# Stick-breaking attention on one core: the mask of the diagonal tiles moves from a matmul into the scores to two elementwise products on the weights

## The chip, the cores and the metric

The kernel runs on one core of a Trainium2 chip. The engines that matter are PE (matmul), DVE (VectorE), ACT (ScalarE) and POOL (GpSimd); SP issues the DMAs. Each engine works through its own instructions in order and waits on semaphores of the others. The metric is the time of one execution in microseconds (us), the median of three runs. The profile is of one further execution, and the prediction's sum is made against that execution's own time.

## The reference, cut to what matters

A layer normalises 2048 tokens (with 16 meta tokens ahead of them), projects them to many channels, and runs three mixers side by side: a stick-breaking attention, a gated delta rule and an HGRN2. Their outputs are gated, projected and added to the input. The change touches the attention alone:

```python
z = einsum('bhqd,bhkd->bhqk', q_block, k[:q1]) * scale
mask = (s_idx < t_idx) & key_valid
log_keep = where(mask, log_sigmoid(-z), 0.0)
log_passed = cumsum(log_keep, reverse=True) - log_keep
attn = where(mask, exp(log_sigmoid(z) + log_passed), 0.0)
out = einsum('bhqk,bhkd->bhqd', attn, v)
```

Each key takes the share sigmoid(z) of what the later keys left over; what a key leaves is the remainder sigmoid(-z). A key at or after the query takes nothing (weight 0) and leaves everything (remainder 1).

## The kernel before

**Tiling.** The tokens are worked in four quarters of 512 (`j` = 0 to 3), four heads in each. Every projection is a sum of three matmuls per 128 rows (`mm3`, L175 to L178: high times high, high times low, low times high), in a 4-byte format, mostly 128x512. These projections (tiles `acc`, from `proj` and `branch`) are the bulk of PE's work and depend on little; below they are called the dense work.

**Attention.** `sb_scan` (L504) does one head of one quarter. Its inner generator `weights` makes one tile for each of the four blocks of 128 queries (`i`) against a range of keys: scores `z` into PSUM (three matmuls), two sigmoids on ACT (L525 the remainders `pc`, L526 the weights `at`), a running product from the last key to the first (L531, a scan on DVE; the next range of keys goes on from its first column, which POOL copies, L530), and the product of weights and scan (L537, on DVE for even `i`, on POOL for odd `i`). Then `values` transposes the four products on PE (L559, tile `tr`), ACT and DVE split them in high and low (L570, L127 through L571), and PE multiplies them with the values (tile `av`). At the end `put_ob` multiplies with the gate (L399) and makes the head's output `ob` (L402), which the branch product (`acc<-ob,w`) needs.

**The mask before.** Where a tile ends with the 128 keys of its own queries (`diag`, one tile per block of queries, 4 in a head, 64 in all), a fourth matmul (L522) adds -1e30 to the scores of the keys at or after the query: `ident_b` times `neg_b`, both bf16, 128x128.

**Order.** `weave` mixes an attention head (or a scan of the other mixers) with steps of dense work as the code is written out; then a scheduler that runs when the kernel is built sets the order of each engine's instructions anew, by its own estimate of how long each takes. So a change of some instructions also moves others on every engine. The buffers are fixed pools: 4 PSUM tiles for `z` and `tr` together, 21 slots "S" for the attention's tiles.

Of the kernel before, what the change touches and what calls it, by code (L numbers as in the profile page):

```python
# [7 lines left out]
F32 = mybir.dt.float32  # L8
F32R = mybir.dt.float32r
BF16 = mybir.dt.bfloat16  # L10
AF = mybir.ActivationFunctionType
ALU = mybir.AluOpType
# [3 lines left out]
P = 128  # L16
# [23 lines left out]
def kernel(  # L40
# [21 lines left out]
    nc = tc.nc  # L62

    const = ctx.enter_context(tc.tile_pool(name="const", bufs=1))
# [19 lines left out]
    def slot(tag, shape=(P, WQ), dt=F32, bufs=None):  # L84
        return pool.tile(list(shape), dt, tag=tag, name=nm(tag), bufs=bufs or BUFS[tag])
# [18 lines left out]
    def p_z():  # L104
        return ps_z.tile([P, 512], F32, tag="z", name=nm("z"))
# [7 lines left out]
    def cload(shape, src, name, dt=F32, eng=None):  # L113
        t = const.tile(list(shape), dt, name=name)
        (eng or nc.sync).dma_start(t, src)
        return t

    nw = cload([P, KC], norm_w, "nw", eng=nc.scalar)
    ident = cload([P, P], c_ident, "ident", eng=nc.scalar)
# [55 lines left out]
    def mm3(dst, lh, ll, rh, rl, first, last):  # L175
        nc.tensor.matmul(dst, lh, rh, start=first, stop=False)  # L176
        nc.tensor.matmul(dst, lh, rl, start=False, stop=False)  # L177
        nc.tensor.matmul(dst, ll, rh, start=False, stop=last)  # L178
# [325 lines left out]
    def sb_scan(j, h, st):  # L504

        qh, ql, kh, kl, vh, vl, vm0, rq, gate = st.pop(h)
# [4 lines left out]
        def weights(s, lo, hi, skh, skl, ats):  # L511
            for i in range(NT):
                e = min(hi, META + (i + 1) * P) if s == j else hi
                if e <= lo:
                    continue
                n = e - lo
                z = p_z()
                diag = s == j and e == META + (i + 1) * P
                qs = slice(META + i * P, META + (i + 1) * P)
                mm3(z[:, :n], qh[:, qs], ql[:, qs], skh[:, lo:e], skl[:, lo:e], True, not diag)  # L520
                if diag:
                    nc.tensor.matmul(z[:, n - P : n], ident_b, neg_b, start=False, stop=True)  # L522
                pc = slot("S")
                at = slot("S")
                nc.scalar.activation(pc[:, :n], z[:, :n], AF.Sigmoid, scale=rq[:, NT + i : NT + i + 1])  # L525
                nc.scalar.activation(at[:, :n], z[:, :n], AF.Sigmoid, scale=rq[:, i : i + 1])  # L526
                if carry[i] is None:
                    nc.gpsimd.memset(pc[:, n : n + 1], 1.0)
                else:
                    nc.gpsimd.tensor_copy(pc[:, n : n + 1], carry[i][:, 0:1])  # L530
                nc.vector.tensor_tensor_scan(  # L531
                    pc[:, 0:n][:, ::-1], pc[:, 0:n][:, ::-1], zero1.broadcast_to([P, n]),
                    1.0 if carry[i] is None else pc[:, n : n + 1], ALU.mult, ALU.add,
                )
                carry[i] = pc
                eng = nc.gpsimd if i % 2 else nc.vector
                eng.tensor_mul(at[:, :n], at[:, :n], pc[:, 1 : n + 1])  # L537
                ats[i] = at
                yield 0.4 + n * 0.0045
# [41 lines left out]
        for s in range(j, -1, -1):  # L581
            vm = vm0
            if s == j:
                skh, skl, svh, svl = kh, kl, vh, vl
            else:
                cs = 0 if s == 0 else META
                skh = slot("S", dt=F32R)
                skl = slot("S", dt=F32R)
# [10 lines left out]
            for lo, hi in [(META + 2 * P, WQ), (0, META + 2 * P)] if s == 0 else [(META, WQ)]:  # L599
                ats = {}  # L600
                now = weights(s, lo, hi, skh, skl, ats)
                if before is None:
                    yield from now
                else:
                    yield from alternate(now, before)
                if lo == 0:
                    work.append((lo, ats, 0, 32, None))
                for kt in range(NT):
                    if lo <= META + kt * P < hi:
                        work.append((lo, ats, META + kt * P, P, kt))  # L610
                if s == j == 0 and lo > 0:
                    continue
                if s == j:
                    work.sort(key=lambda w_: -1 if w_[4] == 0 else (0 if w_[4] is None else w_[4]))
                before = values(s, work, svh, svl, vm, lo == 0)
                work = []
# [818 lines left out]
    with tc.issue_after(marks["act"]), tc.issue_after(marks["dve"]), tc.issue_after(marks["pool"]):  # L1435
        neg32 = slot("D")
# [7 lines left out]
        lbl = cload([P, H], lb_logits, "lbl")  # L1444
        h_on = cload([P, 1], hg_on, "h_on")

        ident_b = const.tile([P, P], BF16, name="ident_b")
        nc.vector.tensor_copy(ident_b, ident)
        neg_b = const.tile([P, P], BF16, name="neg_b")
        nc.vector.tensor_copy(neg_b, neg32[:, :P])  # L1450
        ident4 = const.tile([P, NT, P], F32, name="ident4")
        for n in range(NT):
            nc.gpsimd.tensor_copy(ident4[:, n], ident)
# [153 lines left out]
```

## Time and profile before

| | |
|---|---|
| three runs | 2731.2, 2731.36, 2727.7 us; median 2731.2 us |
| the profiled execution | 2731.59 us; from its first to its last instruction 2729.8 us |
| granted TensorE clock | 0.998 of full speed |
| busy | PE 99%, DVE 52%, ACT 35%, POOL 26% |

PE counts as busy where any matmul is under way; consecutive matmuls overlap in the records, so the time that a matmul takes from PE is the distance from its start to the next start, not its duration. An idle time in brackets names what ended it.

### The profile page before, as it was taken

How to read it: one execution, taken by the hardware profiler on the slowest of the kernel's cores; microseconds unless marked ns; L12 is line 12 of the kernel's file. 1: busy time of each engine (PE TensorE's matmuls, PEld its weight loads, DVE VectorE, ACT ScalarE, POOL GpSimd, SP SyncE). 2: the span in 40 equal slices, each digit the busy share in tenths (PEclk: the TensorE clock that was granted, in tenths of full speed). 3: DMA queues.
4: the chain of work that ended last, by engine and by line, in shares of the span. 5: the costliest groups of instructions: out<-in, count | busy, mean ns of one | idle time of the engine just before them, and what ended most of it. 6: DMA issues, size and time to landing. Idle time of an engine off the chain costs nothing.

```text
span 2729.8 us, 46703 instructions
## 1 busy us (share of the span) xinstructions
PE 2693.7 (99%) x17984; PEld 2245.8 (82%) x17984; DVE 1433.1 (52%) x2878; ACT 960.2 (35%) x2207; POOL 718.8 (26%) x990
## 2 busy tenths in 40 slices
PE   7999999999999999999999999999999999999999
PEld 7998788888888888888888888888888887787887
DVE  5466647745357634443255765553325568556422
ACT  5564343343346212212144641321214456313120
POOL 4555213333133401112122332111212233302111
PEclk9999999999999999999999999999999999999999
DMA  7677756679654654557755456355764454554556
GB/s 261 221 235 251 250 184 221 231 268 319 197 180 146 206 176 130 157 160 242 230 188 171 156 171 203 107 156 155 253 217 142 163 169 142 161 161 121 162 162 212
DMA packets 201986, 521.08 MB, mean 191 GB/s; under 512 B 42976, under 2 KB 47008, under 8 KB 201764
## 3 DMA queue, kind: packets, MB, share of 16 engines
q1 hardware_dynamic: 201476, 518.03, 59.1%
q8 instruction: 142, 2.33, 0.3%
q14 instruction: 80, 0.66, 0.1%
q10 hardware_dynamic: 288, 0.07, 0.0%
HBM read 397.57 MB, written 120.44 MB: 190 GB/s over the span
## 4 chain that ended last, share of the span: by engine, by line
PE 93%; DVE 4%; DMA 1%; ACT 1%; issue 1%; POOL 0%; SPq 0%; DVEq 0%; POOLq 0%; ACTq 0%
PE acc L176 20%; PE acc L177 20%; PE acc L178 20%; PE av L176 5%; PE av L177 5%; PE av L178 5%; PE tr L559 2%; PE t L381 2%; PE z L1152 1%; PE z L176 1%; PE z L177 1%; PE z L178 1%; PE tr L381 1%; PE z L856 1%; PE tr L1237 1%
## 5 line engine op out<-in xcount | busy, mean ns | idle before, releaser
L176 PE MATMUL acc<-xh,w 128*128 128x512 f32 (+2 forms) x2096 | 796.8, 380 | 5.6 <-DVE y L1285 1.7
L177 PE MATMUL acc<-xl,w 128*128 128x512 f32 (+2 forms) x2096 | 790.7, 377 | 0.3 <-DVE xl L261 0.3
L178 PE MATMUL acc<-xh,w 128*128 128x512 f32 (+2 forms) x2096 | 787.1, 376 | 0.5 <-DVE w L127 0.5
L176 PEld LDWEIGHTS acc<-xh,w 128*128 128x128 f32 x2096 | 396.6, 189 | 75.2 <-DVE y L1285 2.1
L178 PEld LDWEIGHTS acc<-xh,w 128*128 128x128 f32 x2096 | 396.6, 189 | 66.8 <-DVE w L127 0.7
L177 PEld LDWEIGHTS acc<-xl,w 128*128 128x128 f32 x2096 | 396.4, 189 | 65.0 <-DVE xl L261 1.1
L531 DVE TENSOR_TENSOR_SCAN S<-S,zero 128x128 f32<-128x128 f32 (+4 forms) x216 | 199.1, 924 | 115.3 <-ACT S L525 105.1
L127 POOL TENSOR_TENSOR w<-wraw,w 128x512 fp32r<-128x512 f32 x106 | 147.0, 1390 | 236.2 <-ACT w L156 227.7
L537 POOL TENSOR_TENSOR S<-S,S 128x256 f32<-128x256 f32 (+2 forms) x108 | 96.5, 893 | 366.6 <-DVE S L531 196.6
L176 PE MATMUL av<-xh,w 128*128 128x512 f32 (+2 forms) x440 | 172.7, 392 | 0.0
L177 PE MATMUL av<-xl,w 128*128 128x512 f32 (+2 forms) x440 | 171.8, 390 | 0.0
L178 PE MATMUL av<-xh,w 128*128 128x512 f32 (+2 forms) x440 | 171.3, 389 | 0.0
L156 ACT CAST w<-wraw 128x512 fp32r<-128x512 f32 x182 | 112.5, 619 | 143.7 <-PE acc L178 69.9
L525 ACT ACTIVATE S<-z,rq 128x128 f32<-128x128 f32 (+4 forms) x216 | 117.1, 542 | 117.7 <-PE z L178 90.6
L737 DVE SCALAR_TENSOR_TENSOR D<-D,cw,D 128x512 f32<-128x512 f32 (+1 forms) x144 | 119.7, 838 | 21.3 <-ACT D L735 19.8
L127 DVE TENSOR_TENSOR S<-tr,S 128x512 fp32r<-128x512 f32 (+4 forms) x176 | 105.9, 606 | 42.5 <-ACT S L564 24.0
L1289 POOL TENSOR_TENSOR y<-y,g 128x512 f32<-128x512 f32 x32 | 48.2, 1506 | 288.8 <-DVE g L1287 288.8
L176 PE MATMUL acc<-ob,w 128*128 128x512 f32 x296 | 118.2, 400 | 1.4 <-ACT ob L402 1.4
L177 PE MATMUL acc<-ob,w 128*128 128x512 f32 x296 | 117.7, 398 | 0.0
L178 PE MATMUL acc<-ob,w 128*128 128x512 f32 x296 | 117.5, 397 | 0.0
L526 ACT ACTIVATE S<-z,rq 128x128 f32<-128x128 f32 (+4 forms) x216 | 116.8, 541 | 0.0
L133 POOL TENSOR_SCALAR nu<-nv 128x8 f32<-128x8 f32 (+3 forms) x39 | 14.8, 379 | 334.9 <-DVE nv L1057 194.4
(404 smaller groups left out, 4980.3 us busy)
## 6 DMA issues: line engine op xcount, KB each, us to landing
w<-wk SPq DMA_DIRECT2D x555, 512.0 KB, 3.6
wk<-w SPq DMA_DIRECT2D x184, 512.0 KB, 3.5
wraw<-in_w_in_dram SPq DMA_DIRECT2D x142, 256.0 KB, 4.0
D<-in_xq_dram SPq DMA_DIRECT2D x56, 256.0 KB, 4.4
S<-rows SPq DMA_DIRECT2D x48, 256.0 KB, 5.1
S<-dv SPq DMA_DIRECT2D x48, 256.0 KB, 4.7
out_dram<-D SPq DMA_DIRECT2D x32, 256.0 KB, 4.7
S<-dk SPq DMA_DIRECT2D x24, 264.0 KB, 3.9
```

The lines of the kernel that those rows point to most:

```text
L127: (eng or nc.gpsimd).tensor_sub(out_, a, hi.bitcast(F32))
L156: nc.scalar.copy(hi, raw)
L176: nc.tensor.matmul(dst, lh, rh, start=first, stop=False)
L177: nc.tensor.matmul(dst, lh, rl, start=False, stop=False)
L178: nc.tensor.matmul(dst, ll, rh, start=False, stop=last)
L381: nc.tensor.transpose(pt[:, n * P : (n + 1) * P], src[:, META + n * P : META + (n + 1) * P], ident)
L525: nc.scalar.activation(pc[:, :n], z[:, :n], AF.Sigmoid, scale=rq[:, NT + i : NT + i + 1])
L526: nc.scalar.activation(at[:, :n], z[:, :n], AF.Sigmoid, scale=rq[:, i : i + 1])
L531: nc.vector.tensor_tensor_scan(pc[:, 0:n][:, ::-1], pc[:, 0:n][:, ::-1], zero1.broadcast_to([P, n]), 1.0 if carry[i] is None else pc[:, n ...
L537: eng.tensor_mul(at[:, :n], at[:, :n], pc[:, 1 : n + 1])
L559: nc.tensor.transpose(tr[:kw, i * P : (i + 1) * P], ats[i][:, a - lo : a - lo + kw], ident)
L737: nc.vector.scalar_tensor_tensor(dst[:, c0:], raw[:, c0 + i : c0 + i + n], cw[:, ci, i : i + 1], dst[:, c0:], ALU.mult, ALU.add)
```

## The change

The fourth matmul is gone, and the third of the scores closes the sum. After the sigmoids, DVE takes the maximum of the last 128 columns of the remainders and a constant that is 1 at the masked keys (`later01`), and POOL multiplies the last 128 columns of the weights by its complement (`upto01`). The two constants are 4-byte tiles made once at the start, in place of the two bf16 ones.

```diff
@@ sb_scan / weights
-                mm3(z[:, :n], qh[:, qs], ql[:, qs], skh[:, lo:e], skl[:, lo:e], True, not diag)
-                if diag:
-                    nc.tensor.matmul(z[:, n - P : n], ident_b, neg_b, start=False, stop=True)
+                mm3(z[:, :n], qh[:, qs], ql[:, qs], skh[:, lo:e], skl[:, lo:e], True, True)
                 pc = slot("S")
                 at = slot("S")
                 nc.scalar.activation(pc[:, :n], z[:, :n], AF.Sigmoid, scale=rq[:, NT + i : NT + i + 1])
                 nc.scalar.activation(at[:, :n], z[:, :n], AF.Sigmoid, scale=rq[:, i : i + 1])
+                if diag:
+
+                    nc.vector.tensor_tensor(pc[:, n - P : n], pc[:, n - P : n], later01, ALU.max)
+                    nc.gpsimd.tensor_mul(at[:, n - P : n], at[:, n - P : n], upto01)
@@ constants at the start
-        ident_b = const.tile([P, P], BF16, name="ident_b")
-        nc.vector.tensor_copy(ident_b, ident)
-        neg_b = const.tile([P, P], BF16, name="neg_b")
-        nc.vector.tensor_copy(neg_b, neg32[:, :P])
+        later01 = const.tile([P, P], F32, name="later01")
+        nc.vector.tensor_scalar(later01, neg32[:, :P], -1.0, 1.0, ALU.mult, ALU.min)
+        upto01 = const.tile([P, P], F32, name="upto01")
+        nc.vector.tensor_scalar(upto01, later01, -1.0, 1.0, ALU.mult, ALU.add)
```

The lines behind the edit move by two: after the change the scan is L533, the product L539, the transposing matmul L561.

Where the instructions stand now is shown at three places. The first is DVE at the start of the second head of the second quarter (`S_1690`, `S_1699` and `S_1702` are the remainders of query blocks 0, 1 and 2, `S_1691` and `S_1703` the weights that DVE multiplies). Before:

```order
L531 SCALAR_TENSOR_TENSOR S_1690_8694<-S_1690_8694,zero1_417 128x128
L537 TENSOR_TENSOR S_1691_8695<-S_1691_8695,S_1690_8694 128x128
L531 SCALAR_TENSOR_TENSOR S_1699_8720<-S_1699_8720,zero1_417 128x256
L531 SCALAR_TENSOR_TENSOR S_1702_8738<-S_1702_8738,zero1_417 128x384
L537 TENSOR_TENSOR S_1703_8739<-S_1703_8739,S_1702_8738 128x384
```

And after, on DVE at the same place:

```order
L527 TENSOR_TENSOR S_1690_8713<-S_1690_8713,later01_408 128x128
L533 SCALAR_TENSOR_TENSOR S_1690_8713<-S_1690_8713,zero1_417 128x128
L527 TENSOR_TENSOR S_1699_8740<-S_1699_8740,later01_408 128x128
L539 TENSOR_TENSOR S_1691_8714<-S_1691_8714,S_1690_8713 128x128
L533 SCALAR_TENSOR_TENSOR S_1699_8740<-S_1699_8740,zero1_417 128x256
L527 TENSOR_TENSOR S_1702_8759<-S_1702_8759,later01_408 128x128
L533 SCALAR_TENSOR_TENSOR S_1702_8759<-S_1702_8759,zero1_417 128x384
L539 TENSOR_TENSOR S_1703_8760<-S_1703_8760,S_1702_8759 128x384
```

A maximum stands ahead of each scan, and nothing else was put between.

The second place is PE at the start of the second head of the last quarter, behind the scores of query blocks 1 to 3 (`z_4136`, `z_4139`, `z_4142`); `acc` tiles are dense work, and `tr_4152` is the first transposed tile of the head. Before:

```order
L178 MATMUL z_4142_21758<-D_4002_21211,D_3973_21095 128x512
L522 LDWEIGHTS ident_b_408
L522 MATMUL z_4142_21758<-neg_b_410,ident_b_408 128x128
L176 MATMUL acc_4293_22347<-xh_3927_20844,w2_4292_22345 128x512
L177 MATMUL acc_4293_22347<-xl_3928_20845,w2_4292_22345 128x512
L178 MATMUL acc_4293_22347<-xh_3927_20844,w2_4292_22345 128x512
L381 MATMUL t_4316_22450<-ident_83,D_4253_22197 128x128 x4
L176 MATMUL acc_4329_22486<-xh_3885_20578,w2_4327_22482 128x512
L177 MATMUL acc_4329_22486<-xl_3886_20579,w2_4327_22482 128x512
L178 MATMUL acc_4329_22486<-xh_3885_20578,w2_4327_22482 128x512
```

After, on PE (`S_4138` is the product for query block 1, made on POOL):

```order
L178 MATMUL z_4136_21781<-D_4002_21263,D_3973_21144 128x256
L176 MATMUL z_4139_21797<-D_4002_21263,D_3972_21143 128x384
L177 MATMUL z_4139_21797<-D_4003_21264,D_3972_21143 128x384
L178 MATMUL z_4139_21797<-D_4002_21263,D_3973_21144 128x384
L176 MATMUL z_4142_21813<-D_4002_21263,D_3972_21143 128x512
L177 MATMUL z_4142_21813<-D_4003_21264,D_3972_21143 128x512
L178 MATMUL z_4142_21813<-D_4002_21263,D_3973_21144 128x512
L177 MATMUL acc_4293_22404<-xl_3928_20893,w2_4292_22402 128x512
L178 MATMUL acc_4293_22404<-xh_3927_20892,w2_4292_22402 128x512
L176 MATMUL z_4149_21840<-S_4145_21832,D_3972_21143 128x512
L561 MATMUL tr_4152_21854<-ident_83,S_4129_21762 128x128
L561 MATMUL tr_4152_21854<-ident_83,S_4138_21786 128x128
```

The first two transposing matmuls now stand two dense matmuls behind the scores; before, 25 dense ones and four transposes of another tile stood there (the rows above show the first of them).

The third place is PE near the end of the last head of the last quarter, around the score tile `z_4542`, which five more follow. Before, one 128x512 matmul of a long row of dense work ahead of it, and what follows:

```order
L178 MATMUL acc_4741_24356<-xh_3927_20844,w2_4740_24354 128x512
L381 MATMUL t_4747_24403<-ident_83,D_4716_24226 128x128 x4
L176 MATMUL z_4542_23351<-S_4521_23283,D_4288_22340 128x256
L177 MATMUL z_4542_23351<-S_4522_23284,D_4288_22340 128x256
L178 MATMUL z_4542_23351<-S_4521_23283,D_4289_22341 128x256
L176 MATMUL av_4440_22947<-S_4534_23318,S_4491_23150 128x512
L177 MATMUL av_4440_22947<-S_4535_23319,S_4491_23150 128x512
L178 MATMUL av_4440_22947<-S_4534_23318,S_4492_23151 128x512
```

After, on PE at the same place:

```order
L177 MATMUL z_4526_23357<-S_4522_23348,D_4288_22397 128x256
L178 MATMUL z_4526_23357<-S_4521_23347,D_4289_22398 128x256
L177 MATMUL z_4536_23386<-S_4522_23348,D_4288_22397 128x256
L178 MATMUL z_4536_23386<-S_4521_23347,D_4289_22398 128x256
L178 MATMUL acc_4748_24476<-ob_4438_22996,w2_4736_24399 128x512
L176 MATMUL z_4542_23415<-S_4521_23347,D_4288_22397 128x256
L177 MATMUL z_4542_23415<-S_4522_23348,D_4288_22397 128x256
L178 MATMUL z_4542_23415<-S_4521_23347,D_4289_22398 128x256
L176 MATMUL av_4440_23007<-S_4534_23382,S_4491_23214 128x512
L177 MATMUL av_4440_23007<-S_4535_23383,S_4491_23214 128x512
L178 MATMUL av_4440_23007<-S_4534_23382,S_4492_23215 128x512
```

Before, 17 dense matmuls and the four transposes of `t_4747` stand between the last matmul of `z_4526` and the end of the head; after, one dense matmul does. The other 16, the four transposes and five transposes of the attention's own stand ahead of it.

## Rows read from the trace of the kernel before

**Rows 1.** The page's first part: busy time of each engine, its share of the span, instructions.

```profile
span 2729.8 us, 46703 instructions
PE 2693.7 (99%) x17984; PEld 2245.8 (82%) x17984; DVE 1433.1 (52%) x2878; ACT 960.2 (35%) x2207; POOL 718.8 (26%) x990
```

**Rows 2.** The page's fourth part: the chain of work that ended last, by engine.

```profile
PE 93%; DVE 4%; DMA 1%; ACT 1%; issue 1%; POOL 0%; SPq 0%; DVEq 0%; POOLq 0%; ACTq 0%
```

**Rows 3.** All instructions of line 522, the mask: engine, operation, count, shortest, median and longest duration in ns; below, who waited for it (us, times).

```profile
L522 PE MATMUL z<-neg_b,ident_b x64: 229/230/234, 56.5 to 2275.8; 128*128 128x128 bf16 x64
...
  ACT S L525: 22.7, 11
```

**Rows 4.** PE's instructions in order of time around two masks, in the first quarter and in the last: start in us, duration, line, tiles, shape.

```profile
58.79 0.28 PE L178 MATMUL z<-D,D 128*128 128x256 f32 x1
58.91 0.23 PE L522 MATMUL z<-neg_b,ident_b 128*128 128x128 bf16 x1
58.95 0.48 PE L176 MATMUL acc<-xh,w 128*128 128x512 f32 x1
59.27 0.39 PE L177 MATMUL acc<-xl,w 128*128 128x512 f32 x1
59.50 0.39 PE L178 MATMUL acc<-xh,w 128*128 128x512 f32 x1
...
2275.51 0.40 PE L178 MATMUL z<-D,D 128*128 128x512 f32 x1
2275.75 0.23 PE L522 MATMUL z<-neg_b,ident_b 128*128 128x128 bf16 x1
2275.79 0.48 PE L177 MATMUL acc<-xl,w 128*128 128x512 f32 x1
2276.11 0.39 PE L178 MATMUL acc<-xh,w 128*128 128x512 f32 x1
```

**Rows 5.** PE in order of time where a transposing matmul follows the mask (the last of the masks of a head of the first quarter).

```profile
88.84 0.23 PE L522 MATMUL z<-neg_b,ident_b 128*128 128x128 bf16 x1
88.91 0.27 PE L483 MATMUL t<-ident,D 128*16 128x128 f32 x1
88.94 0.48 PE L176 MATMUL acc<-xh,w 128*128 128x512 f32 x1
```

**Rows 6.** Groups of instructions by line, engine, operation and shape: busy us, mean ns of one, idle time before them and what ended it. The steps of an attention tile, and the one POOL operation that reads 128x128.

```profile
L537 DVE TENSOR_TENSOR S<-S,S 128x128 f32<-128x128 f32 x16 | 4.6, 289 | 1.7
L531 DVE TENSOR_TENSOR_SCAN S<-S,zero 128x256 f32<-128x256 f32 x64 | 47.4, 741 | 41.2 <-ACT S L525 37.8 <-ACT S L526 3.3
L525 ACT ACTIVATE S<-z,rq 128x256 f32<-128x256 f32 x64 | 30.7, 480 | 58.0 <-PE z L178 35.7 <-PE z L522 19.5 <-PE av L177 2.0
L537 POOL TENSOR_TENSOR S<-S,S 128x256 f32<-128x256 f32 x40 | 32.9, 823 | 165.5 <-DVE S L531 68.8 <-ACT S L525 54.7 <-ACT D L418 13.8
L1453 POOL COPY ident<-ident 128x128 f32<-128x128 f32 x4 | 1.4, 402 | 0.0
```

**Rows 7.** The 108 products of weights and scan on POOL, all shapes: shortest, median and longest duration in ns.

```profile
L537 POOL TENSOR_TENSOR S<-S,S x108: 632/674/1483, 60.6 to 2335.8; 128x256 f32<-128x256 f32 x40, 128x512 f32<-128x512 f32 x36, 128x272 f32<-128x272 f32 x32
```

**Rows 8.** Busy time in stretches of the span: length, then busy us (instructions) of PE, PEld, DVE, ACT, POOL, then granted clock, DMA share, GB/s. The first two rows are the last two heads of the last quarter, the third the end of the last of them, then the attention of the third, second and first quarter.

```profile
2200.00:2274.00 74.00, 72.62 (x377) 59.62 (x377) 59.95 (x93) 45.03 (x93) 25.69 (x44) 1.00 0.47 152
2274.00:2350.00 76.00, 70.02 (x363) 56.27 (x362) 58.91 (x93) 43.64 (x94) 27.36 (x42) 0.98 0.43 138
2321.87:2342.30 20.43, 17.55 (x91) 13.30 (x89) 13.09 (x23) 11.88 (x29) 3.43 (x10) 0.92 0.31 91
1355.00:1620.00 265.00, 265.00 (x1377) 220.04 (x1377) 163.13 (x266) 137.61 (x285) 71.39 (x142) 1.00 0.52 171
700.00:890.00 190.00, 190.00 (x1014) 158.91 (x1013) 116.40 (x200) 100.07 (x217) 55.96 (x109) 1.00 0.54 172
56.00:188.00 132.00, 131.94 (x944) 122.40 (x944) 71.84 (x128) 76.82 (x178) 71.15 (x96) 1.00 0.67 229
```

**Rows 9.** PE in order of time, its waits near the end of the third head of the last quarter; in brackets the idle time and what ended it.

```profile
2254.67 0.50 PE L177 MATMUL av<-S,S 128*128 128x512 f32 x1 [0.46 <-DVE S L127]
...
2256.70 0.66 PE L381 MATMUL t<-ident,D 128*128 128x128 f32 x4 [0.69 <-ACT D L759]
...
2257.90 0.50 PE L177 MATMUL av<-S,S 128*128 128x512 f32 x1 [0.23 <-DVE S L127]
```

**Rows 10.** The same for the end of the last head of the last quarter, PE and DVE, from the scan that follows `z_4526` (2321.87) on.

```profile
2321.87 0.74 DVE L531 TENSOR_TENSOR_SCAN S<-S,zero 128x256 f32<-128x256 f32 x1
...
2325.58 0.75 DVE L531 TENSOR_TENSOR_SCAN S<-S,zero 128x256 f32<-128x256 f32 x1 [0.56 <-ACT S L525]
...
2328.86 0.75 DVE L531 TENSOR_TENSOR_SCAN S<-S,zero 128x256 f32<-128x256 f32 x1 [1.40 <-ACT S L525]
...
2336.01 1.03 PE L559 MATMUL tr<-ident,S 128*32 128x128 f32 x6 [0.76 <-DVE S L537]
...
2339.04 0.67 PE L548 MATMUL av<-S,vmp 96*128 96x512 f32 x1 [2.00 <-ACT S L566]
...
2342.30 0.69 DVE L399 TENSOR_TENSOR S<-av,D 128x512 f32<-128x512 f32 x1 [2.84 <-PE av L178]
...
2343.69 0.73 PE L176 MATMUL acc<-ob,w 128*128 128x512 f32 x2 [1.43 <-ACT ob L402]
...
2349.30 0.50 PE L176 MATMUL acc<-xh,w 128*128 128x512 f32 x1 [1.71 <-DVE y L1285]
```

## The prediction

> **What bounds the kernel now.** I read the page's busy times first, then the chain of waits, then the mask's own line, then PE in order of time. PE is busy for 2693.7 of 2729.8 us, the next engine for half [rows 1], and 93% of the chain that ended last is PE [rows 2]. Through the attention of the first three quarters PE is busy in every microsecond but 0.06 (132 of 132, 190 of 190, 265 of 265 us), while DVE stays near 60% and POOL under 55% [rows 8]. There a matmul that goes is time that goes, and a delay on another engine costs nothing as long as dense work stands in front of the matmul that waits. In the last quarter this ends: in the stretch of the third head PE misses 1.4 us and in that of the fourth 6.0 us, with DVE at 60 of 74 and 59 of 76 us [rows 8]. Its waits there name DVE and ACT: three at the end of the third head [rows 9], and at the end of the fourth 0.76, 2.00, 1.43 and 1.71 us, when the dense work that needs nothing from the attention has run out [rows 10]. So the change has to be priced twice: by what PE no longer does, and by what its new order does to the last quarter.
>
> **What goes.** The 64 masks have a duration of 0.23 us each [rows 3], but matmuls overlap, so I take distances from start to start. In the first quarter the score's last matmul starts at 58.79, the mask at 58.91, the next dense matmul at 58.95 and the one behind it at 59.27 [rows 4]. From 58.79 to 59.27 are 0.48 us. Without a mask the 128x256 matmul takes 0.12 (58.79 to 58.91) and a dense one 0.23 (59.27 to 59.50), together 0.35: the mask costs 0.13 us, of which only 0.04 are its own slot and 0.09 are lost by the matmul behind it. In the last quarter 2275.51 to 2276.11 is 0.60 us against two times 0.23, 0.14 by these rounded starts [rows 4]. I take 0.13. In five of the 64 places a transposing matmul follows, and mask and transpose together take 0.10 us (88.84 to 88.94) [rows 5]; I book nothing there. 59 times 0.13 is 7.7 us. All of it stands on the chain, except where PE waits anyway, which is near none of the masks: they stand at the starts of heads, from 56.5 to 2275.7 [rows 3], and the waits at their ends. The bounds are 64 times 0.04 = 2.6 us, if the next matmul lost its 0.09 for another reason (a change of weights that comes anyway), and 64 times 0.13 = 8.3 us.
>
> The Trainium skill, page "TensorE: Matmul & The Clock Gate", section "Back-to-back issue gap", gives about 81 ns for a 128-column matmul with its weight load in a stream. By it the masks would give back 64 times 0.081 = 5.2 us; the rows show 130 ns where a 2-byte matmul stands between 4-byte ones, and I go by the rows.
>
> **What comes, and what hides it.** DVE gets 64 maxima of 128x128, both inputs in SBUF: 0.29 us each by the product of the same shape [rows 6], 18.5 us in all. POOL gets 64 products of 128x128. The trace has none of that shape: a copy of it took 0.40, a product of twice the columns 0.82 on the mean [rows 6]; nearer to both is 0.5, 32 us in all. On a path a diagonal tile gets longer by the maximum, 0.3 us, since POOL's mask runs while DVE scans for 0.74 [rows 6]; where the scan is not what POOL's product waits for, up to 0.8. ACT in turn starts earlier by the mask's 0.04 to 0.13. In the first three quarters the cover is dense work: by the new order of PE and the spacings of rows 4, at least 5 us of matmuls stand between a diagonal tile's scores and its first transpose, against a path of two sigmoids, maximum, scan and product, 0.48 + 0.29 + 0.74 + 0.82 = 2.3 us and the hops between them. I cost it at nothing; without that cover it would be 0.3 to 0.8 us per head. The two constants at the start replace two DVE instructions by two: nothing.
>
> **What moves.** In the last quarter three places count.
>
> First, the start of the second head. Behind the last score matmul of query block 1 there now stand only three of 384 columns, three of 512, two dense ones and one score matmul ahead of the two transposes: 3 times 0.17 (my estimate, three quarters of 0.23), 6 times 0.23, 1.9 us. The path to `S_4138` on POOL is the 2.3 us above plus the matmul's drain and the hops, some 2.8 us. PE waits about 0.8 us where it did not before. Bounds: 0, if the hops are short, and 2, if POOL comes late.
>
> Second, the end of the third head: its waits of 0.46, 0.69 and 0.23 us [rows 9] lie in a stretch into which the new order puts 16 dense matmuls (3.7 us). I take 1.2 us back; bounds 1.4 and minus 1 (the same waits at other instructions).
>
> Third, the end of the last head. In the new order 16 dense matmuls (3.7 us) and nine transposes (1.0 us) that stood within it stand ahead of it, so its last six tiles start 4.7 us later against the rest of the order. In return the path through them is no longer held up. From the scan at 2321.87 to the last product at 2342.30 are 20.4 us. DVE is busy for 13.1 of them [rows 8], and of its waits two at the end stay (for the last transposes, and 2.84 for the `av` matmuls). The hold-ups that can go are DVE's 1.40 before the scan of 2328.86, which waits for scores behind nine dense matmuls, 0.56 of the same kind at the scan of 2325.58, and, my estimate, about 0.5 ahead of 2321.87 [rows 10]. That is 2.5 us back for 4.7 us later: 2.2 us lost. Bounds: 0, if all of it comes back, and 4.7, if nothing does. The granted clock is 0.92 of full in this stretch against 1.00 before it [rows 8]; the waits that go before its fall are the ones that stay, so I add nothing for it.
>
> The sum: -7.7 - 1.2 + 0.8 + 2.2 = -5.9 us, on the profiled 2731.59 us, which makes 2725.7. The profiled execution lies 0.4 us above the median of 2731.2, so against the median I forecast 2725.3 us, 0.22% less. A measurement of this kernel can tell about 0.2%, 5.5 us, from no change, so the forecast lies just beyond that mark.
>
> **Rivals.** *The order takes most of it back.* The last head loses its full 4.7, the second its 2, and the third's waits come back: -7.7 + 4.7 + 2 = -1 us, 2730. For it: PE waits there already [rows 10], and the order is made by an estimate that did not foresee these waits. Against it: DVE's waits in rows 10 do show a hold-up that the move ends.
>
> *PE gains more.* The masks' full 8.3 us, the third head's 1.4, no loss at the end: -9.7 us, 2721.5. For it: in most of the span nothing else waits. Against it: 4.7 us of filler do leave a stretch that has nothing to fill it.
>
> *Slower: DVE and POOL get in each other's way.* POOL's products of one kind range from 632 to 1483 ns, at three shapes, but the median is 674 with a third of them 512 wide [rows 7], and the mean for 256 columns, 823, is above that for the median of all: POOL's time does not follow the size alone. If the new maximum and the new POOL mask, which start within a sigmoid of each other on each of the 64 tiles, each wait out the other, the path of a diagonal tile grows by 0.3 + 0.5 + 0.3 = 1.1 us. In the last quarter, where DVE is at 80%, 16 tiles would put 17 us on four heads, and the first 6 or so would vanish behind dense work: -7.7 + 11 + 2 = +5, 2736. It decides from the point at which the heads of the last quarter finish 8 us later against the dense work. Against it: the masks stand at a head's start, where the dense work is thickest. The Trainium skill speaks for this rival: "SBUF — State Buffer", section "Who interferes with whom", says that a DVE instruction with two SBUF inputs contends with a GpSimd instruction that reads SBUF, and that the later of the two waits out the other; the spread of POOL's durations agrees, though no row here shows two such instructions against each other.
>
> That the masks don't go can be left out: the new order has no L522.
>
> **How the numbers follow.** My forecast, with its own range of 2722 to 2729, gets 0.62; the order that takes it back 0.19; the greater gain 0.10; slower 0.09. Of the forecast's 0.62 two thirds lie beyond the mark of 0.2%, which with the greater gain gives 0.51 for faster. The rest of the forecast and the order that takes it back give 0.40 for no difference, and 0.09 is left for slower. The range goes from 2719, below the greater gain since the masks' cost is read from a few starts, to 2732, which takes in the order that takes it back and leaves out most of the slower rival.
>
> **What would show it.** Right: PE's busy time falls by some 8 us; behind `z`'s third matmul of a diagonal tile the next starts with no 0.09 lost; the maxima take 0.29 us; in the first three quarters PE stays busy throughout; the wait of the last head's end grows from 6 to about 8 us in all. Wrong: PE idle in the first three quarters behind transposes that wait for L539 on POOL; POOL's masks longer than 0.8 us; or the last head's end no later, or 5 us later, against the dense work.

## The result: 0.26% slower, and the profile after

The changed kernel takes 2736.1 us, the median of 11 runs, against 2729.0 for the kernel before on the same chip: a ratio of 1.0026, with a 95% interval of 1.0018 to 1.0034. That is 7.2 us more, where 5.9 less had been forecast; 2736.1 lies outside the range of 2719 to 2732.

Busy times and chain of the page after, for [rows 1] and [rows 2]:

```profile
span 2734.3 us, 46658 instructions
PE 2690.1 (98%) x17920; PEld 2242.8 (82%) x17920; DVE 1466.2 (54%) x2942; ACT 959.1 (35%) x2207; POOL 745.4 (27%) x1054
...
PE 90%; DVE 6%; DMA 1%; ACT 1%; issue 1%; POOL 1%; SPq 0%; DVEq 0%; POOLq 0%; ACTq 0%
```

PE works 3.6 us less and waits 8.1 us more (44.2 against 36.1 us idle in the span); DVE's share of the chain grew. The stretches of [rows 8] tell where:

```profile
2200.00:2274.00 74.00, 71.90 (x371) 59.12 (x370) 56.43 (x87) 41.02 (x83) 21.57 (x40) 1.00 0.45 144
2274.00:2350.00 76.00, 64.28 (x316) 50.45 (x315) 55.98 (x91) 41.95 (x87) 23.85 (x40) 0.96 0.37 116
...
1355.00:1620.00 265.00, 264.83 (x1372) 220.49 (x1372) 170.14 (x282) 136.78 (x283) 77.42 (x155) 1.00 0.52 170
...
700.00:890.00 190.00, 190.00 (x1007) 159.64 (x1006) 128.18 (x223) 100.25 (x219) 67.04 (x129) 1.00 0.53 173
...
56.00:188.00 132.00, 131.08 (x934) 121.31 (x933) 82.80 (x146) 76.58 (x175) 81.83 (x112) 1.00 0.67 229
```

In the first three quarters PE stays busy to within 0.9 us in each stretch, though DVE got 7 to 12 us more in each stretch and POOL 6 to 11. In 2274 to 2350 it loses 5.7 us more than before. Who made PE wait in the last quarter's attention (line waited at, releaser, us in all, times, longest):

```profile
PE t L381 <- ACT D L761: 2.6, 1, 2.6
PE tr L561 <- POOL S L539: 2.2, 3, 1.0
PE av L550 <- ACT S L568: 2.0, 1, 2.0
PE av L177 <- DVE S L127: 1.8, 3, 0.9
PE acc L176 <- DVE y L1287: 1.7, 1, 1.7
PE z L176 <- DVE S L127: 1.7, 1, 1.7
PE av L176 <- ACT S L572: 1.5, 2, 1.3
PE acc L176 <- ACT ob L402: 1.4, 1, 1.4
PE tr L561 <- DVE S L539: 0.8, 1, 0.8
...
```

The 2.0, 1.7, 1.4 and 0.8 us are those of [rows 10], unchanged. The others are new or longer, and about half of them by time (single waits of 2.65, 1.27 and 1.01 us) stand at the start of the fourth head.

A second count needs one mark: DVE's product with the gate (L399), with which a head ends. What is said below to be "at the marks" is read from one profiled execution of each kernel, and executions of one kernel differ by some us. Between these marks the next view counts PE's dense matmuls (tile `acc`) alone: length of the head, busy us (matmuls), granted clock, DMA share, GB/s, for heads 2, 3 and 4 of the last quarter. First before, then after:

```profile
2117.55:2200.12 82.57, 58.20 (x225) 1.00 0.48 158
2200.12:2274.47 74.35, 45.59 (x176) 1.00 0.47 153
2274.47:2342.30 67.83, 36.47 (x140) 0.98 0.45 144
```

```profile
2110.52:2192.04 81.52, 55.76 (x213) 1.00 0.49 156
2192.04:2273.33 81.29, 53.70 (x209) 1.00 0.48 152
2273.33:2346.98 73.65, 32.52 (x118) 0.95 0.39 123
```

At the end of the second head the changed kernel leads by 8.1 us (2192.04 against 2200.12), and at the end of the fourth it is 4.7 late. The third head got 33 more dense matmuls and takes 6.9 us more. The fourth has 22 fewer, 5.1 us of PE's work, and yet takes 5.8 us **more**.

### The profile page after: what moved, and what is told of

It is laid out like the page before. It is cut to its first block, busy times and chain, and to the rows that moved or that the text cites. A ratio compares the mean times of both kernels' runs of the same rounds, so it can differ in the third digit from the quotient of the medians.

```text
span 2734.3 us, 46658 instructions
## 1 busy us (share of the span) xinstructions
PE 2690.1 (98%) x17920; PEld 2242.8 (82%) x17920; DVE 1466.2 (54%) x2942; ACT 959.1 (35%) x2207; POOL 745.4 (27%) x1054
## 4 chain that ended last, share of the span: by engine, by line
PE 90%; DVE 6%; DMA 1%; ACT 1%; issue 1%; POOL 1%; SPq 0%; DVEq 0%; POOLq 0%; ACTq 0%
PE acc L176 20%; PE acc L177 19%; PE acc L178 19%; PE av L176 5%; PE av L177 5%; PE av L178 5%; PE tr L561 2%; PE t L381 2%; PE z L1154 1%; PE z L178 1%; PE z L177 1%; PE z L176 1%; PE z L858 1%; PE tr L381 1%; DVE D L739 1%
## 5 line engine op out<-in xcount | busy, mean ns | idle before, releaser
L533 DVE TENSOR_TENSOR_SCAN S<-S,zero 128x128 f32<-128x128 f32 (+4 forms) x216 | 203.7, 944 | 86.1 <-ACT S L523 77.7
L539 POOL TENSOR_TENSOR S<-S,S 128x256 f32<-128x256 f32 (+2 forms) x108 | 91.0, 843 | 287.7 <-DVE S L533 203.5
L561 PE MATMUL tr<-ident,S 128*128 128x128 f32 (+1 forms) x608 | 102.6, 272 | 3.1 <-POOL S L539 2.2
```

The lines of the kernel that those rows point to most:

```text
L533: nc.vector.tensor_tensor_scan(pc[:, 0:n][:, ::-1], pc[:, 0:n][:, ::-1], zero1.broadcast_to([P, n]), 1.0 if carry[i] is None else pc[:, n ...
L561: nc.tensor.transpose(tr[:kw, i * P : (i + 1) * P], ats[i][:, a - lo : a - lo + kw], ident)
```

## The experiments

**How the order was held.** A change of one instruction makes the scheduler order all five engines anew. To part the order from the instructions, the kernels below carry a table of each engine's order and tie every instruction behind the one that the table puts ahead of it. Ties add no instruction. That they cost no time by themselves can be seen further below: mix_spliced_order is tied and mix_own_order is not, PE's order is the same in both but for 35 of 17936 matmuls, and they measure 0.9988 and 0.9989. The new masks are left out of the table and stand where the scheduler finds room; a matmul mask is tied behind its scores. In the names, `mm` is the mask as a matmul, `ew` maximum and product, `no` no mask and `mix` a kernel with both kinds; `before_order` and `after_order` say whose order it has.

```diff
+    def pin_order():
+        for eng, code in ORDER.items():
...
+            for s_ in steps.tolist():
+                at += 1 + s_
+                if prev is not None:
+                    tc.add_manual_dep(
+                        mine[at], prev.name,
+                        mybir.DependencyInfo(mybir.DependencyClass.NoSync, mybir.DependencyReason.DATA),
+                        reason="order",
+                    )
+                prev = mine[at]
```

**Instructions and order apart.** Three ways to mask (a matmul, nothing, maximum and product) in two orders (before's, the changed kernel's): two of the six are the kernels themselves, four were run. Theory A: the order makes the loss. Theory B: the new instructions do. The edit of those without a mask, against the changed kernel:

```diff
-                if diag:
-
-                    nc.vector.tensor_tensor(pc[:, n - P : n], pc[:, n - P : n], later01, ALU.max)
-                    nc.gpsimd.tensor_mul(at[:, n - P : n], at[:, n - P : n], upto01)
```

> The changed kernel (maximum on DVE, product on POOL), with every other instruction of all five engines pinned to the order in which the kernel before has them; the new instructions are left where the scheduler finds room. Theory A (the new order puts dense work ahead of the last quarter's attention, and that alone costs the 13 us by which PE's waits grew): the masks' 7 to 8 us come back and nothing is lost, 0.9972 of the kernel before, PE's waits in the last quarter near its 7 us. Theory B (maximum and mask lie on the path of the diagonal tiles, and DVE and POOL hold each other up): the waits stay in the last quarter with the old order too, 1.001 to 1.003. Half of each would be 0.9995.

> The kernel before (mask as a matmul, no maximum, no product), with every instruction pinned to the order of the changed kernel, each mask directly behind the third matmul of its scores. Theory A: the waits of the changed kernel stay, and the masks' matmuls come on top, 1.005 (some 14 us slower than before). Theory B: the waits go with the new instructions, 1.000 to 1.001.

> No mask at all (the masking of the diagonal tiles is left out: no matmul, no maximum, no product), in the order of the kernel before. It measures the masks' matmuls alone. Prediction's term: -7.7 us, 0.9972. If the next matmul loses its 0.09 us for another reason, -2.6 us, 0.999. Both theories expect the same here; theory A expects the run ew_before_order within 1 us of this one, theory B 8 to 12 us above it.

> No mask at all (the masking of the diagonal tiles is left out), in the order of the changed kernel. Theory A: as slow as the changed kernel within 2 us, 1.002 to 1.003, since the order makes the waits. Theory B: the waits go with the new instructions, 0.997 to 0.998, as without masks in the old order.

Measured, as ratios to the kernel before (95% intervals of about 0.0009 either way, 0.0013 for mm_after_order):

| | before's order | changed kernel's order |
|---|---|---|
| mask as a matmul | 1 | 1.0036 |
| no mask | 0.9983 | 1.0018 |
| maximum and product | 1.0007 | 1.0026 |

Read down, the masks' matmuls are worth 0.0017 to 0.0018, 4.6 to 4.9 us. Read across, the order costs 0.0035 and 0.0036 (some 9.7 us) without the new instructions, and 0.0019 with them; that the new order hides part of the new instructions would explain it, but the difference of 0.0016 is hardly clear of the intervals. Down again, the new instructions cost 0.0024 (6.5 us) in the old order and 0.0008 (2.2 us) in their own; the second is within the intervals, and at the marks the last three heads take 2.8 us more with them (236.5 against 233.7). The changed kernel is the sum -4.6 + 9.6 + 2.2 = 7.2 us, each term uncertain by some 3 us. Theory A has most of the changed kernel's loss, though mm_after_order stays below its 1.005; ew_before_order came out where theory B put it, not at theory A's 0.9972. There the cover of the dense work fails in the second quarter, whose heads take 3.6 us more from the first mark to the last than without masks (135.1 against 131.5), and 4.7 us more stand in the last quarter's three heads (229.3 against 224.5); the first and the third quarter differ by 0.5 us at most. Waits of PE from 700 to 890 us, and one of the four places:

```profile
PE tr L573 <- POOL S L551: 2.3, 4, 0.8
```

```profile
804.03 1.10 POOL L551 TENSOR_TENSOR S<-S,S 128x512 f32<-128x512 f32 x1 [1.70 <-DVE S L545]
...
805.18 0.55 PE L573 MATMUL tr<-ident,S 128*128 128x128 f32 x3 [0.61 <-POOL S L551]
```

The transpose waits for POOL's product, which waited 1.70 us for the scan.

**What a mask was worth.** With the same order on PE, each mask's cost is the difference of two distances. At the place of [rows 4], without a mask:

```profile
57.79 0.29 PE L187 MATMUL z<-D,D 128*128 128x256 f32 x1
57.91 0.39 PE L185 MATMUL acc<-xh,w 128*128 128x512 f32 x1
58.14 0.39 PE L186 MATMUL acc<-xl,w 128*128 128x512 f32 x1
```

From 57.79 to 58.14 are 0.35 us against 0.48: 0.13, as read. But behind scores of 128 columns, first with the mask, then without:

```profile
2107.61 0.27 PE L178 MATMUL z<-D,D 128*128 128x128 f32 x1
2107.73 0.23 PE L522 MATMUL z<-neg_b,ident_b 128*128 128x128 bf16 x1
2107.77 0.48 PE L177 MATMUL acc<-xl,w 128*128 128x512 f32 x1
2108.09 0.39 PE L178 MATMUL acc<-xh,w 128*128 128x512 f32 x1
```

```profile
2103.29 0.28 PE L187 MATMUL z<-D,D 128*128 128x128 f32 x1
2103.41 0.44 PE L186 MATMUL acc<-xl,w 128*128 128x512 f32 x1
2103.69 0.39 PE L187 MATMUL acc<-xh,w 128*128 128x512 f32 x1
```

0.48 against 0.40 us: the dense matmul behind a short one loses 0.05 without a mask too. Over all 64 places the difference is on the mean 0.125 to 0.13 us behind 256 columns and more (41 places), 0.075 to 0.08 behind 128 or 144 (18), and between 0.00 and 0.07 where a transpose follows (5): 6.8 us in all. In the second and third quarter the kernel without masks keeps what this adds up to (1.8 and 1.7 us over the attention of each); in heads 2 to 4 of the last quarter, between whose marks 11 masks add up to 1.3 us, it keeps 0.2 (224.5 against 224.8 us), where PE waits for the attention.

**Maximum or product.** One of the two alone, in before's order:

```diff
-                    nc.gpsimd.tensor_mul(at[:, n - P : n], at[:, n - P : n], upto01)
```

> Only the maximum on DVE, no product on POOL (the weights of masked keys are not set to zero), in the order of the kernel before. Compared with no_before_order (0.9983) and ew_before_order (1.0007), which are 6.5 us apart by these ratios: theory C (POOL's product is the dear one: it stands ahead of the next product on POOL, and DVE's product waits for it) expects 0.9987 or less; theory D (the maximum is the dear one: it stands ahead of the scan on the path and waits out POOL, up to 1.3 us where 0.28 is its own) expects 1.000 or more.

```diff
-                    nc.vector.tensor_tensor(pc[:, n - P : n], pc[:, n - P : n], later01, ALU.max)
```

> Only the product with the mask on POOL, no maximum on DVE (the remainders of masked keys are not set to one), in the order of the kernel before. Theory C: 1.000 or more. Theory D: 0.9987 or less. If the two cost only together, both runs are at 0.9985.

Measured 0.9991 (0.9982 to 0.9999) and 0.9999 (0.9990 to 1.0008). Against 0.9983 without a mask, the maximum costs 0.0008 and the product 0.0016, and together they make up the 0.0024. The product is the dearer, as theory C had it, though neither number reaches the mark that C had named, and an interval of 0.0009 hardly parts the two.

**The last quarter's order alone.** A table that holds the changed kernel's order up to the fourth quarter's projections, and before's from there; then the same with the matmul mask in the last quarter:

```diff
-                mm3(z[:, :n], qh[:, qs], ql[:, qs], skh[:, lo:e], skl[:, lo:e], True, True)
+                mm3(z[:, :n], qh[:, qs], ql[:, qs], skh[:, lo:e], skl[:, lo:e], True, not (diag and j == nq - 1))
+                if diag and j == nq - 1:
+                    e1 = nc.tensor.matmul(z[:, n - P : n], ident_b, neg_b, start=False, stop=True)
...
-                if diag:
...
+                if diag and not j == nq - 1:
```

> The changed kernel, pinned to its own order until the fourth quarter's projections, and from there to the order of the kernel before. If the order of the last quarter is what the changed kernel lost by: it keeps the 7 to 8 us by which it leads at 2060 us, and loses to the new instructions alone, some 2 us, in the last heads: 0.9975 to 0.9985. If the lead at 2060 us is only dense work done earlier that is missing later: 1.000 to 1.001, as ew_before_order.

> Maximum and product in the first three quarters, mask as a matmul in the last; pinned to the changed kernel's order in the first three and to the order of the kernel before in the last. If the new instructions cost something only where PE waits for the attention (the last quarter), it is the fastest of all: 0.997 to 0.9975, 7 to 8 us less. If they cost nothing there either, it is slower than ew_spliced_order by the last quarter's 16 masks, 1.5 us.

Measured 1.0001 (0.9992 to 1.0010) and 0.9988 (0.9979 to 0.9997). The old order in the last quarter alone gives back 0.0025, 6.8 us, so the loss of the order lies there. Both stay short of what was expected if it lay there alone (0.9975 to 0.9985, and 0.997 to 0.9975). The first has the time named for the other reading, dense work that is missing later, but not for that reason: its three last heads have before's count of dense matmuls (225, 176, 140), and yet take 228.7 us at the marks, 3.9 more than before's 224.8, which is the new instructions. With the matmul mask in the last quarter they take 224.9, and the kernel is 0.12% faster than before.

**Which part of that order.** In the changed kernel the last head's keys and values are loaded (SP's queue, `S<-dk`) two, two and one weight loads later than before, and 20 of PE's dense matmuls stand ahead of the fourth head's scores that stood behind them. Five kernels move one or both of these, with everything else tied. In the lines below a name with x3 stands for three matmuls of that tile.

```diff
 # ew_sp_back: the changed kernel, SP of the last quarter as before
-ORDER["SP"] = changed
+ORDER["SP"] = changed up to the fourth quarter, before behind it
 # mm_sp_late: the kernel before, SP of the last quarter as changed
 # ew_dense_behind: the changed kernel, on PE
-z_4448 x3, dense x20, av_4284 x7, z_4451 x3, z_4454 x3, dense x4
+z_4448 x3, av_4284 x7, z_4451 x3, z_4454 x3, dense x24
 # ew_both_back: ew_sp_back and ew_dense_behind
 # mm_both_moved: the kernel before, on PE, and its first key group two weight loads later on SP
-av_4284 x2, z_4448 x1, ..., z_4454 x3, dense x26
+dense x20, av_4284 x2, z_4448 x1, ..., z_4454 x3, dense x6
```

> The changed kernel in its own order on PE, DVE, ACT and POOL; SP's DMA queue alone is pinned, from the fourth quarter's projections on, to the order of the kernel before. That moves the three groups of key and value loads of the last head two, two and one weight loads earlier in SP's queue. Theory S (the weight loads wait for buffers that dense matmuls free, and the last head's keys wait behind them on SP, so its scores come late): the keys are issued 5 to 9 us earlier against the head's start, DVE's 5.3 us of idle time before a late scan shrinks to 1 or 2, and 5 to 8 us come back of the changed kernel's 1.0026: 0.9997 to 1.0008. Theory P (the place of the dense matmuls in PE's own queue makes the waits): as the changed kernel, 1.002 to 1.003, and the key loads themselves then wait on SP.

> The kernel before in its own order on PE, DVE, ACT and POOL; SP's DMA queue alone is pinned, from the fourth quarter's projections on, to the order of the changed kernel, which puts the last head's key and value loads two, two and one weight loads later. Theory S: the loss of the order appears without any other change, 1.002 to 1.004. Theory P: 1.000.

> The changed kernel in its own order on every engine, but for one block on PE in the last quarter: 20 dense matmuls (4.6 us), which its order puts ahead of the third head's last products and of the fourth head's scores of query blocks 2 and 3, stand behind these scores, where the kernel before has 26 dense ones. Theory P (the waits come from where the dense matmuls stand on PE): the third head ends 4.6 us earlier, the waits of 1.0, 2.65 and 1.27 us at the start of the fourth go, and 4 to 8 us of the changed kernel's 7 come back: 0.9996 to 1.0011. Theory D2 (it is DVE's work and the buffers of the last head, wherever the dense matmuls stand): the waits come back a few us later, 1.002 to 1.003.

> The changed kernel with both moves of ew_dense_behind and ew_sp_back: 20 dense matmuls stand behind the fourth head's first scores, and SP's queue of the last quarter has the order of the kernel before. If the two belong together (the dense matmuls free the weight buffers, the weight loads stand ahead of the key loads): 4 to 7 us less than the changed kernel, 1.0000 to 1.0012. If the rest of the order, which the two moves leave, holds the last head up by itself: 1.002 to 1.003.

> The kernel before, with nothing changed but two places of the last quarter: 20 dense matmuls (4.6 us) pulled ahead of the third head's last products and the fourth head's scores, and that head's first group of key and value loads two weight loads later on SP, as the changed kernel has them. If these two places make the loss: 1.002 to 1.0035. If the rest of the order makes it: 1.000 to 1.001.

| | ratio | 95% interval | heads 2, 3, 4 in us | dense matmuls |
|---|---|---|---|---|
| before | 1 | | 82.6, 74.4, 67.8 | 225, 176, 140 |
| changed | 1.0026 | 1.0018 to 1.0034 | 81.5, 81.3, 73.7 | 213, 209, 118 |
| ew_sp_back | 1.0041 | 1.0028 to 1.0054 | 81.5, 82.0, 74.3 | 213, 209, 118 |
| ew_dense_behind | 1.0025 | 1.0014 to 1.0036 | 81.5, 77.1, 77.0 | 213, 189, 138 |
| ew_both_back | 1.0019 | 1.0010 to 1.0028 | 81.7, 79.2, 73.4 | 213, 189, 138 |
| mm_sp_late | 1.0050 | 1.0037 to 1.0063 | 82.5, 74.7, 81.2 | 225, 176, 140 |
| mm_both_moved | 1.0019 | 1.0011 to 1.0028 | 82.5, 79.1, 67.0 | 225, 196, 120 |

The clearest is mm_both_moved, heads 3 and 4 in the count of dense matmuls:

```profile
2195.27:2274.32 79.05, 50.26 (x196) 1.00 0.48 153
2274.32:2341.33 67.01, 31.83 (x120) 0.99 0.42 136
```

The third head takes 20 dense matmuls more and 4.7 us more. The fourth takes 20 fewer, and is shorter by 0.8 us only. Its length is not PE's: the dense matmuls in it filled waits, and taken out of it they cost their full time elsewhere. This makes 3.8 us at the marks and 0.0019 in the ratio, half of the order's 0.0035. The key loads were moved too and not parted from the matmuls here, but no wait of PE in these heads names a load.

The other half is left to the rest of the order. SP can make such a loss, and a larger one than theory S named: in mm_sp_late PE waits 6.9 us for the keys, whose loads stand behind weight loads that wait for PE (SP's queue, then PE):

```profile
2288.89 8.81 SPq L158 DMA_DIRECT2D w<-wk  x3
2297.79 0.86 SPq L606 DMA_DIRECT2D S<-dk  x2
```

```profile
2301.37 0.79 PE L185 MATMUL z<-S,D 128*128 128x512 f32 x1 [3.85 <-DMA S<-dk]
```

In the changed kernel the second group of keys comes late as well, 28.5 us after the third head's end (2301.86) where before it was 17.8 (2292.24). But theory S falls with ew_sp_back: earlier in the queue, they wait there themselves, from 2289.85 to 2302.86, and hold up the weight loads behind them:

```profile
2286.06 3.79 SPq L158 DMA_DIRECT2D w<-wk  x2
2302.86 0.79 SPq L607 DMA_DIRECT2D S<-dk  x2
```

Who released that load (line waited at, releaser, us, times, longest):

```profile
SPq L607 <- PE av L185: 13.2, 1, 13.2
```

An `av` matmul reads tiles of the pool "S", from which the keys take their buffers; so the likeliest reason is a buffer that the late attention still holds. Theory P falls with ew_dense_behind, whose 1.0025 is theory D2's figure: the 20 matmuls, back in the fourth head, make the third 4.2 us shorter and the fourth 3.3 longer, so in the new order they fill few waits. Neither move alone gave anything back, and both together 0.0007 at most, within the intervals. So the 20 matmuls and the key loads are enough to make half the loss in the old order, but not the whole cause in the new one; what else lengthens its last head (73.4 us in ew_both_back against 70.2 in ew_spliced_order, with 138 and 140 dense matmuls) was not parted further. One candidate is seen: DVE's wait of 5.3 us near the end of that head is there in all kernels of the table that keep the changed kernel's end of the head (5.2 to 5.3), and without masks in that order (5.4), and is 1.4 in ew_spliced_order. No run moved it alone.

**A version without ties.** The mixed mask of mix_spliced_order, in whatever order the scheduler makes:

> Maximum and product in the first three quarters, mask as a matmul in the last, in whatever order the scheduler makes of it, nothing pinned. In its SP queue the last head's key loads stand where the kernel before has them. Theory S: it keeps what mix_spliced_order showed, 0.998 to 0.9995, the first three quarters' masks less and no new waits in the last. Theory P: between 0.998 and 1.002, by where the dense matmuls fall.

Measured 0.9989 (0.9980 to 0.9998), 3.0 us less than before: it beats both kernels, by little. Its last heads have before's count:

```profile
2192.96:2267.31 74.35, 45.53 (x176) 1.00 0.48 153
2267.31:2334.03 66.72, 36.45 (x140) 1.00 0.47 147
```

## Why the prediction was wrong, point by point

**What goes: right in kind, too large.** 7.7 us were forecast, 6.8 measured over the 64 places and 4.6 to 4.9 kept; PE's busy time, which was to fall by some 8 us, fell by 3.6. The 0.13 holds where the scores have 256 columns or more, which is where it was read; behind 128 or 144 columns the next matmul loses 0.05 without a mask too, as the lower bound had allowed for; that the reason is "a change of weights that comes anyway" is not shown. And that PE's waits are "near none of the masks" does not help: what the masks free in the last quarter's heads is lost again before their end (0.2 of 1.3 us kept). The lower figure of the Trainium skill (page "TensorE: Matmul & The Clock Gate", section "Back-to-back issue gap"; 5.2 us) is nearer to what was kept than the row, but as a cost per mask the mean of 0.106 us lies between its 0.081 and the 0.13.

**What comes: right for the median, too small in sum, and not nothing.** The two new lines (engine, operation, count, shortest, median and longest in ns; then busy us and mean ns of one):

```profile
L527 DVE TENSOR_TENSOR S<-S,later x64: 256/283/1383, 55.0 to 2280.0; 128x128 f32<-128x128 f32 x64
...
L528 POOL TENSOR_TENSOR S<-S,upto x64: 453/512/1378, 56.1 to 2279.5; 128x128 f32<-128x128 f32 x64
...
L527 DVE TENSOR_TENSOR S<-S,later 128x128 f32<-128x128 f32 x64 | 28.3, 445 | 7.5 <-ACT S L523 7.5
...
L528 POOL TENSOR_TENSOR S<-S,upto 128x128 f32<-128x128 f32 x64 | 40.6, 638 | 78.3 <-ACT S L524 78.3
```

The medians are 0.28 and 0.51 us against 0.29 and 0.5; the sums are 28 and 41 us against 18.5 and 32 (for DVE, which waits out POOL, see the last section), and 16 of POOL's 64 are longer than the 0.8 us that the prediction named as a sign of being wrong. The cover of the first three quarters held to within 1 us in the changed kernel's own order and fails in the second quarter in the old one, so it is the scheduler's work. In the last quarter there is no such cover, and the 2.2 us are left (2.8 at the marks), which the sum had at nothing beyond the 0.8. Part of it may be PE's clock: in the fourth head, which takes 1.9 us more than without masks in the same order (73.65 against 71.77), the granted clock is 0.95 against 0.98; the two were not parted.

**What moves, first and second place: right in kind.** The second head's transposes wait 0.75 us for POOL (0.8 forecast); by the count of dense matmuls, without a mask on either side, that head loses 2.0 us, the upper bound (12 fewer, 2.8 us, and 0.8 us shorter):

```profile
2113.92 0.33 PE L561 MATMUL tr<-ident,S 128*128 128x128 f32 x1 [0.75 <-POOL S L539]
```

At the third head 16 more dense matmuls were forecast to end its waits and to give 1.2 us back. Without a mask in the new order it has 33 more, 7.6 us, and takes 6.0 more than in the old: 1.6 back, a little beyond the bound of 1.4.

**What moves, third place: the step that failed.** "In return the path through them is no longer held up ... That is 2.5 us back for 4.7 us later: 2.2 us lost." Nothing came back. Without masks on either side the fourth head has 22 fewer dense matmuls (5.1 us) and takes 71.8 us against 67.8: 9.1 us lost where 2.2 stood. The bound of 4.7 is what moved matmuls cost when nothing comes back; mm_both_moved, which moves 20 others, loses 3.8 of their 4.6 us. It was no bound for the order as a whole, of which only the end of the head was priced. New waits are at its start, where PE waits to transpose another mixer's tile, whose operand comes late from DVE and ACT behind an attention scan of 2.12 us, and then for ACT again (without masks in the same order the first of these two waits is 1.2 us):

```profile
2283.52 2.12 DVE L533 TENSOR_TENSOR_SCAN S<-S,zero 128x512 f32<-128x512 f32 x1
...
2288.21 0.66 PE L381 MATMUL t<-ident,D 128*128 128x128 f32 x4 [2.65 <-ACT D L761]
...
2290.13 0.79 PE L176 MATMUL av<-S,D 128*128 128x512 f32 x1 [1.27 <-ACT S L572]
```

And the hold-ups of DVE that were to go came back larger: 5.30 us ahead of the scan for `z_4526`, where [rows 10] had 1.40 and 0.56 ahead of later scans. They had been read wrongly, too. The 1.40 is not a wait for scores behind nine dense matmuls: these scores start at 2325.12 to 2325.44, ahead of the nine, and ACT's sigmoid waits for an `av` matmul behind them, likeliest for a buffer "S" that it frees. The 0.56 is no such wait either; ACT was busy with another mixer's tile (2323.98 to 2325.11). It is in the changed kernel that the scores stand behind dense matmuls, eight of them. ACT's wait before, then after, and DVE's after:

```profile
2328.29 0.47 ACT L525 ACTIVATE S<-z,rq 128x256 f32<-128x256 f32 x1 [1.96 <-PE av L177]
...
2328.67 0.47 ACT L523 ACTIVATE S<-z,rq 128x256 f32<-128x256 f32 x1 [2.84 <-PE z L178]
...
2329.24 0.75 DVE L533 TENSOR_TENSOR_SCAN S<-S,zero 128x256 f32<-128x256 f32 x1 [5.30 <-ACT S L523]
```

SP's queue, in which the keys of that head had moved behind further weight loads, was left out of the prediction. So the step that failed is the return of 2.5 us, with a bound taken from the end of one head; what stood in its place is 9.1 us lost in that head. About half of what the order costs is traced to moved dense matmuls and key loads (mm_both_moved); the cause of the other half stays open.

**The rivals.** "The order takes most of it back" had the right mechanism, with 6.7 us for an order that costs 9.6. "Slower" had the right time, 2736, and its mechanism is real, but it carries 2.2 of the 11.8 us lost against the masks' 4.6; the rest is the order. That its time came out is luck.

## What to carry to other kernels

Where a scheduler orders the program, a change is two changes: price the instructions, and count the filler work between fixed marks on the critical engine, stage by stage, before and after; work that fills waits is free only where it stands, and here cost nearly its full time when it was moved out. Look at the queue of loads in the same way, since a load that waits for a buffer holds up all that is behind it. And when one engine has no idle time in most of the program and waits in one stage, use the cheaper variant by stage: here the elementwise mask in the first three quarters and the matmul in the last.

## What the runs showed of the hardware

The maximum on DVE takes 0.28 us, never over 0.292, in the 20 of 64 cases in which POOL has no product or subtraction under way, and 0.52 on the mean in the other 44. The five longest, 1.22 to 1.38 us, each end 0.15 us behind an instruction of POOL that started first (DVE, then POOL, of the changed kernel):

```profile
802.62 1.31 DVE L527 TENSOR_TENSOR S<-S,later 128x128 f32<-128x128 f32 x1
```

```profile
801.84 1.93 POOL L127 TENSOR_TENSOR ob<-S,ob 128x512 fp32r<-128x512 f32 x1
```

DVE's ends at 803.93, POOL's at 803.77, and the maximum lasts 1.0 us beyond its own time. The Trainium skill, page "SBUF — State Buffer", section "Who interferes with whom", says that of two such instructions the later waits out the other; the trace agrees here.
